# Up products of a two-layer trunk with the tokens stationary instead of the weights, and their turn by way of DRAM

## The chip, the core and the metric

The kernel runs on one core of a Trainium2 chip. The metric is the device time in microseconds from the start to the end of one execution. Every time here is of that kind, or of a stretch inside one profiled execution. TensorE multiplies: each matmul holds a 128 x 128 *stationary* tile and streams a *moving* tile of up to 512 columns past it, and the result lands in PSUM. VectorE and ScalarE work on SBUF and PSUM. SP issues the DMA transfers.

## The reference, cut to what matters

Two layers work on 256 tokens of width 2048. Layer 0 has forgetting attention, layer 1 dilated attention; each mixer and each MLP is preceded by an RMSNorm and adds into the residual stream. All data are float32.

```python
def sq_relu_mlp(h, w_up, w_down):
    a = jax.nn.relu(h @ w_up)          # (256, 2048) @ (2048, 8192)
    return (a * a) @ w_down            # (256, 8192) @ (8192, 2048)

for i in range(DEPTH):                 # DEPTH = 2
    h = rms_norm(x, mix_norm_g[i])
    x = x + mixer_i(h)                 # fox_attention, dilated_attention
    h = rms_norm(x, mlp_norm_g[i])
    x = x + sq_relu_mlp(h, mlp_w_up[i], mlp_w_down[i])
```

## The kernel before, in words

**Precision.** A float32 product is made of three products of rounded parts: every operand is split into a high part `hi` (a cast to the matmul's own 32-bit type `F32R`) and a rest `lo`, and hi·hi + hi·lo + lo·hi is summed in PSUM. Weights are split on the chip: `load` brings two row blocks of 128 x 512 (512 KB) into a `raw` tile; `split_part` casts them on ScalarE (L328, `wh`) and subtracts on VectorE (L329, `wl`). There are five `raw` tiles and five pairs of split tiles. A split is emitted when TensorE's program has used the oldest pair, and the next load when a `raw` tile has been split. The order of all weights is a list, `plan`, written to match the order of the products.

**Steps.** A *product* has 512 output columns and 16 steps, one for each 128 rows of the contraction. Each step ends in `jobs.tick()`. Everything that isn't a product's matmul (norms, the heads' softmax, what follows a product) is a generator; `yield 3` lets it go on three steps later, and `yield key` when another has set that key. `clear(n)` is n or n + 1, whichever makes the step odd. `need(key)` ticks on until the key is set. After each tick `pin` ties each engine's instructions to the order in which they were emitted, so this order is the program's order on every queue, SP's included. `in_group` runs some products in parts: with `PARTS` = (0, 12), (12, 16) and two products it does steps 0 to 11 of each, then 12 to 15 of each.

**Products with tokens stationary.** `product_steps` (L353) takes, per step and for each of two blocks of 128 tokens, three matmuls of 512 columns: token parts stationary, weight parts moving (L363 to L365). The result has tokens on the partitions, in two PSUM banks. All products but the MLP's up products are made so.

**The MLP.** `mlp` (L924) goes through four blocks of 2048 hidden columns: four up products, then four down products that contract these 2048 columns and add into `x` (`out_proj`, `add_chain`, L862). The down products want the hidden values with the hidden column on the partitions. Before, the up products deliver them so: `transposed_steps` (L417) holds 128 weight columns stationary and streams the tokens, per step four pairs of a matmul of 512 columns (weight `hi` against both token parts, L429) and one of 256 (weight `lo` against the tokens' `hi`, L433). The result lies in four banks, two of the pool `acc` and two of `sc` or `tp`. `up_chain` (L894) adds the halves of each bank (ScalarE copy L903, VectorE add L904), squares the positive part (L909) and splits it (L912, L913) into `aTh` and `aTl`, tiles of two chunks of 128 hidden columns. In the first block of each MLP the first two up products are a group, because the normalised tokens arrive piece by piece. The four down products follow one another undivided.

**Turning by way of DRAM.** Where tokens must be turned, `transposed_by_dma` (L455) and `qk_chain` (L538) turn 32 x 32 blocks on VectorE (`nc.vector.transpose`, L468, L563), write the 128 x 512 tile to DRAM in four transfers (`move`, L287) that put the blocks in their places, and read it back in one.

Of the kernel before, what the change touches and what calls it, by code (L numbers as in the profile page):

```python
# [17 lines left out]
P = 128  # L18
D = 2048
# [73 lines left out]
def trunk(ctx: ExitStack, tc, x, fox_w_in, fox_b_f, fox_q_gain, fox_k_gain, fox_w_out, dil_w_in,  # L93
# [296 lines left out]
    def last_product(keys, lhs, ready):  # L390
# [7 lines left out]
        for k, x in steps:  # L398
# [13 lines left out]
            if k < KC // 2 and x == len(parts) - 1:  # L412
                if k % W_SUB == W_SUB - 1:
                    split()
                jobs.tick()

    def transposed_steps(banks, keys, both, steps):  # L417


        for k in steps:  # L420
            jobs.need(keys(k))
            i = k % W_SUB
            hi, lo = splits[used[0]]
            tokens = both(k)
            for b in range(NC // P):
                col = slice(b * P, (b + 1) * P)

                def main(first, last):
                    nc.tensor.matmul(  # L429
                        banks[b], hi[:, i, col], in_turn(tokens.rearrange("p x s -> p (x s)"), P // 2), start=first, stop=last)  # L430

                def rest():
                    nc.tensor.matmul(banks[b][:, 0:S], lo[:, i, col], in_turn(tokens[:, 0, :], P // 2), start=False, stop=False)  # L433

                if k == 0:
                    main(True, False)
                    rest()
                else:
                    rest()
                    main(False, k == KC - 1)  # L440
            if i == W_SUB - 1:
                used[0] += 1
                split()
            jobs.tick()


    hT = {}
# [86 lines left out]
    def keys_h(tag):  # L534
        return lambda k: (tag, k // 2)
# [207 lines left out]
    def fox_head(j, hh, qT, kT, vt):  # L743
        h = 4 * j + hh
        at = ((2, 7, 12, 16) if j == 3 else (3, 8, 18, 22))[hh]
        yield ("fq", j)
        yield "gate"
        yield "mask"
        if hh:
            yield ("fk", j)  # L750
            yield at - 8

        bias = work.tile([P, 3 * P], F32, tag="bias", name=f"bias{h}", bufs=2)
        move(bias, negc[h:h + 1, :].to_broadcast([P, 3 * P]))
# [36 lines left out]


    def dil_head(q4, i, qTs, kTs, vt):
# [31 lines left out]
        yield ("dv", q4)  # L825
        pt_sb = yield from p_split(turned, f"d{h}")
        yield 2 if q4 == 3 else 4
        hi, lo = (act.tile([P, 2, S], F32R, tag=f"aT{x}", name=f"oTd{x}_{h}", bufs=KC // 2) for x in "hl")
        oT["d", h] = hi, lo
        yield from pv(pt_sb, vt, [i * S, i * S + P], [hi[:, 0, :], hi[:, 1, :]], [lo[:, 0, :], lo[:, 1, :]], f"d{h}", int(q4 < 3))  # L830
        jobs.done.add(("od", h))

# [44 lines left out]
            (nc.scalar if cols.start else nc.sync).dma_start(dst[:, :, cols.start // 2:cols.stop // 2], at)  # L877
        return ready

    def out_proj(keys, lhs, then=None, ready=None, scale=None, group=0):  # L880
        posts = [lambda acc, n=n: add_chain(acc, n, then, ready, scale) for n in range(NX)]
        if group:
            in_group(lambda n: sums(*(() if n < 2 else (ps_tp, "tp"))),
                     lambda acc, ks: product_steps(acc, keys, lhs, ks), posts[0:group], OUT_PARTS)
        for n in range(group, NX):
            if ready is not None and n == NX - 1:
                last_product(keys, lhs, final_add(n, scale))
            else:
                product(keys, lhs, posts[n])
# [1 line left out]
    def store(n, t):  # L891
        nc.sync.dma_start(out[0][t * P:(t + 1) * P, n * NC:(n + 1) * NC], xt[n][:, t, :])

    def up_chain(banks, key, n, aT):  # L894

        yield 0
        z = []
        for half in range(2):
            t = work.tile([P, 2, S], F32, tag="w", name=f"z_{key}_{n}_{half}", bufs=6)
            for i in range(2):  # L900
                bank = banks[half * 2 + i]
                at = halves(t[:, i, :], P // 2)
                nc.scalar.copy(at, by_column(bank[:, S:2 * S], P // 2))  # L903
                nc.vector.tensor_add(at, by_column(bank[:, 0:S], P // 2), at)  # L904
            z.append(t)
        for half in range(2):
            pr = n * 2 + half
            a = z[half]
            nc.vector.scalar_tensor_tensor(a, a, 0.0, a, ALU.max, ALU.mult)  # L909
            hi = act.tile([P, 2, S], F32R, tag="aTh", name=f"aTh_{key}_{pr}", bufs=KC // 2)  # L910
            lo = act.tile([P, 2, S], F32R, tag="aTl", name=f"aTl_{key}_{pr}", bufs=KC // 2)
            nc.scalar.copy(hi, a)  # L912
            nc.vector.tensor_sub(lo, a, hi.bitcast(F32))  # L913
            aT[pr] = (hi, lo)
            jobs.done.add((key, pr))
            yield 1

    def up_banks(key, n):

        other = (ps_sc, "sc") if n % 2 == 0 else (ps_tp, "tp")  # L920
        pools = (other, (ps_acc, "acc"))
        return [pool.tile([P, NC], F32, tag=tag, name=f"up_{key}_{n}_{tag}{i}") for pool, tag in pools for i in range(2)]

    def mlp(tag, **after):  # L924
        for b in range(4):
            key = f"{tag}a{b}"
            aT = {}
            posts = [lambda banks, n=n: up_chain(banks, key, n, aT) for n in range(4)]

            def steps(banks, ks):  # L930
                transposed_steps(banks, keys_h(tag), lambda k: hT[tag][k // 2][:, k % 2], ks)

            if b == 0:
                in_group(lambda n: up_banks(key, n), steps, posts[0:2])
            for n in range(0 if b else 2, 4):
                banks = up_banks(key, n)
                steps(banks, range(KC))
                jobs.spawn(posts[n](banks))
            out_proj(lambda k: (key, k // 2),
                     lambda k: (aT[k // 2][0][:, k % 2, :], aT[k // 2][1][:, k % 2, :]),  # L940
                     scale=tag, **(after if b == 3 else {}))

    def normed(tag, col, wait=lambda n: 2, later=lambda n: 2):
        ssp = norm_begin(tag)
# [62 lines left out]
    for j in range(4):  # L1007
# [11 lines left out]
        for hh in range(4):  # L1019
# [1 line left out]
        product(keys_h(tag), lhs_h(tag), lambda acc: v_chain(acc, tag, ("fv", j), vt))  # L1021

    out_proj(lambda k: ("of", k),
             lambda k: (oT["f", k // 2][0][:, k % 2, :], oT["f", k // 2][1][:, k % 2, :]),
             normed("n1", MLP_G), group=3)
    jobs.spawn(dilation_tables())
    mlp("n1", then=normed("n2", KC))
    dilated("n2")
    out_proj(lambda k: ("od", k // 2),
             lambda k: (oT["d", k // 2][0][:, k % 2, :], oT["d", k // 2][1][:, k % 2, :]),  # L1030
             normed("n3", MLP_G + KC), group=3)
    mlp("n3", ready=store)
    while jobs.live:
# [30 lines left out]
```

## Time and profile before

| | us |
|---|---|
| Median of three runs | 2143.05 (2142.60 to 2143.11) |
| Profiled execution | 2142.78 |
| Its span, first to last instruction | 2141.1 |
| One block's four up products (533.38 to 617.22) | 83.84 |
| One block's four down products (450.50 to 533.38) | 82.88 |
| TensorE busy | 2134.4 |
| VectorE busy | 1427.9 |
| ScalarE busy | 1094.9 |

The busy time of TensorE counts from a matmul's start to its modelled end, and these overlap; how fast it works is seen in the distances between starts. Idle time of VectorE, ScalarE or the DMA engines costs nothing by itself. A row of a group reads: line, engine, operation, result and operands, shape, count, then busy time, mean duration of one in ns, and the idle time before it with what ended that. A row of a wait reads: who, waited for whom, us in total, times, longest.

### The profile page before, as it was taken

The page shows a single profiled execution, that of the slowest core. Times are in us where ns is not written, and L with a number is a line of the kernel's source. Part 1 is how long each engine was busy: PE and PEld are TensorE (multiplying, and loading weights), DVE is VectorE, ACT ScalarE, POOL GpSimd, SP SyncE. Part 2 cuts the span into 40 slices and gives each one's busy share as a digit, 9 for nine tenths or more (in the row PEclk, how much of TensorE's full clock was granted, in tenths as well). Part 3 has the DMA queues.
Part 4 walks back from the last instruction along what each step waited for, and adds up shares of the span by engine and source line. Part 5 has one row for each costly group of instructions (what it writes and reads, how often), then busy time and mean ns, then how long its engine had stood idle before and what let it go on. Part 6 is the DMA issues. An engine that isn't in the chain of part 4 may idle for free.

```text
span 2141.1 us, 29878 instructions
## 1 busy us (share of the span) xinstructions
PE 2134.4 (100%) x11100; PEld 1900.5 (89%) x11100; DVE 1427.9 (67%) x1890; ACT 1094.9 (51%) x1523; POOL 49.8 (2%) x46
## 2 busy tenths in 40 slices
PE   9999999999999999999999999999999999999999
PEld 7888888988988998998888888888988988988988
DVE  6888876785665565566668787768655655665664
ACT  6565655644444453455555665646544543444442
POOL 2000000000000000000010010000000000000000
PEclk9999999999999999999999999999999999999999
DMA  7888877766666666657777776868666566666664
GB/s 253 258 260 271 251 243 243 235 212 202 191 211 204 197 206 205 201 188 255 244 238 231 245 242 216 260 202 277 203 204 201 190 214 205 197 206 202 201 212 143
DMA packets 315075, 471.97 MB, mean 220 GB/s; under 512 B 36440, under 2 KB 124848, under 8 KB 314928
## 3 DMA queue, kind: packets, MB, share of 16 engines
q1 hardware_dynamic: 314512, 469.66, 68.7%
q8 instruction: 87, 1.43, 0.3%
q14 instruction: 60, 0.49, 0.1%
q10 hardware_dynamic: 416, 0.39, 0.1%
HBM read 446.35 MB, written 23.62 MB: 219 GB/s over the span
## 4 chain that ended last, share of the span: by engine, by line
PE 99%; ACT 0%; DMA 0%; issue 0%; SPq 0%; DVE 0%; ACTq 0%
PE acc L364 21%; PE acc L363 21%; PE acc L365 21%; PE up_n3a_acc L429 5%; PE up_n1a_acc L429 5%; PE up_n3a_sc L429 3%; PE up_n3a_tp L429 3%; PE up_n1a_sc L429 3%; PE up_n1a_tp L429 3%; PE up_n1a_acc L433 3%; PE up_n3a_acc L433 3%; PE up_n1a_tp L433 1%; PE up_n1a_sc L433 1%; PE up_n3a_tp L433 1%; PE up_n3a_sc L433 1%; PE sc_d L672 0%
## 5 line engine op out<-in xcount | busy, mean ns | idle before, releaser
L329 DVE TENSOR_TENSOR wl<-raw,wh 128x1024 fp32r<-128x1024 f32 (+1 forms) x803 | 969.8, 1218 | 628.2 <-ACT wh L328 620.7
L328 ACT CAST wh<-raw 128x1024 fp32r<-128x1024 f32 (+1 forms) x803 | 830.5, 1044 | 863.5 <-PE acc L365 556.9
L363 PE MATMUL acc<-wh,hT_n 128*128 128x512 f32 x896 | 342.8, 383 | 0.4 <-ACT hT_n L506 0.3
L364 PE MATMUL acc<-wl,hT_n 128*128 128x512 f32 x896 | 339.8, 379 | 0.2 <-DVE wl L329 0.2
L365 PE MATMUL acc<-wh,hT_n 128*128 128x512 f32 x896 | 339.7, 379 | 0.0
L363 PE MATMUL acc<-wh,aTh_n1a 128*128 128x512 f32 x512 | 194.0, 379 | 0.0
L364 PE MATMUL acc<-wl,aTh_n1a 128*128 128x512 f32 x512 | 194.0, 379 | 0.0
L365 PE MATMUL acc<-wh,aTl_n1a 128*128 128x512 f32 x512 | 194.0, 379 | 0.0
L365 PEld LDWEIGHTS acc<-wh,hT_n 128*128 128x128 f32 x896 | 169.3, 189 | 24.2 <-DVE hT_n L507 0.2
L363 PEld LDWEIGHTS acc<-wh,hT_n 128*128 128x128 f32 x896 | 169.5, 189 | 23.4 <-ACT hT_n L506 0.6
L364 PEld LDWEIGHTS acc<-wl,hT_n 128*128 128x128 f32 x896 | 169.5, 189 | 23.1 <-DVE wl L329 0.8
L363 PE MATMUL acc<-wh,aTh_n3a 128*128 128x512 f32 x480 | 181.9, 379 | 0.0
L364 PE MATMUL acc<-wl,aTh_n3a 128*128 128x512 f32 x480 | 181.9, 379 | 0.0
L365 PE MATMUL acc<-wh,aTl_n3a 128*128 128x512 f32 x480 | 181.9, 379 | 0.0
L429 PE MATMUL up_n1a_acc<-hT_n,wh 128*128 128x512 f32 x512 | 181.6, 382 | 0.0
L429 PE MATMUL up_n3a_acc<-hT_n,wh 128*128 128x512 f32 x512 | 181.6, 382 | 0.0
L433 PE MATMUL up_n1a_acc<-hT_n,wl 128*128 128x256 f32 x512 | 139.6, 273 | 0.0
L433 PE MATMUL up_n3a_acc<-hT_n,wl 128*128 128x256 f32 x512 | 139.6, 273 | 0.0
L365 PEld LDWEIGHTS acc<-wh,aTl_n1a 128*128 128x128 f32 x512 | 96.8, 189 | 13.8
L364 PEld LDWEIGHTS acc<-wl,aTh_n1a 128*128 128x128 f32 x512 | 96.8, 189 | 13.7
L363 PEld LDWEIGHTS acc<-wh,aTh_n1a 128*128 128x128 f32 x512 | 96.8, 189 | 13.6
L429 PEld LDWEIGHTS up_n1a_acc<-hT_n,wh 128*128 128x128 f32 x512 | 96.8, 189 | 13.5
(681 smaller groups left out, 3159.9 us busy)
## 6 DMA issues: line engine op xcount, KB each, us to landing
raw<-in_mlp_w_up_dram SPq DMA_DIRECT2D x256, 512.0 KB, 4.3
raw<-in_mlp_w_down_dram SPq DMA_DIRECT2D x256, 512.0 KB, 4.2
raw<-in_dil_w_in_dram SPq DMA_DIRECT2D x192, 256.0 KB, 3.3
raw<-in_fox_w_in_dram SPq DMA_DIRECT2D x95, 512.0 KB, 5.0
raw<-in_fox_w_out_dram SPq DMA_DIRECT2D x32, 512.0 KB, 4.8
raw<-in_dil_w_in_dram SPq DMA_DIRECT2D x32, 512.0 KB, 4.4
raw<-in_dil_w_out_dram SPq DMA_DIRECT2D x32, 512.0 KB, 3.8
blocks_n<-turned_n SPq DMA_DIRECT2D x96, 64.0 KB, 2.4
```

What stands on the lines that cost most here:

```text
L328: nc.scalar.copy(hi[:, part, :], raw[:, part, :])
L329: nc.vector.tensor_sub(lo[:, part, :], raw[:, part, :], hi[:, part, :].bitcast(F32))
L363: nc.tensor.matmul(acc[t], ah[:, tok], hi, start=first, stop=False)
L364: nc.tensor.matmul(acc[t], ah[:, tok], lo, start=False, stop=False)
L365: nc.tensor.matmul(acc[t], al[:, tok], hi, start=False, stop=last)
L429: nc.tensor.matmul(banks[b], hi[:, i, col], in_turn(tokens.rearrange("p x s -> p (x s)"), P // 2), start=first, stop=last)
L433: nc.tensor.matmul(banks[b][:, 0:S], lo[:, i, col], in_turn(tokens[:, 0, :], P // 2), start=False, stop=False)
```

## The change

The up products are made by `product_steps`, as all others: tokens stationary, 512 columns of weights moving. Their result has tokens on the partitions, so `up_chain` now turns it. For each of the two token blocks it takes the positive part out of PSUM and squares it on ScalarE, turns 32 x 32 blocks on VectorE, writes to DRAM in four transfers and reads back in one, then splits it into tiles of four chunks (cast on ScalarE, subtraction on VectorE). The waits between these parts are counted in steps, some 19 from the product's end to the last subtraction. The heads' outputs `oT` share the tiles' tag, so they are kept by four chunks as well. In every block the first two of the four down products become a group in `PARTS`, and the list of weights follows. Only the `acc` pool's four banks serve the up products.

```diff
@@ add_mlp
-            for n in range(NX):
-                add(mlp_w_down[l], (b * D, (b + 1) * D), [(n * NC, NC)])
+            down = mlp_w_down[l][b * D:(b + 1) * D]
+            add_group(*((down, [(n * NC, NC)]) for n in range(2)))
+            for n in range(2, NX):
+                add(down, (0, D), [(n * NC, NC)])
@@
-    def transposed_steps(banks, keys, both, steps):
...
@@ fox_head (dil_head alike)
-        if ("f", h // 2) not in oT:
-            oT["f", h // 2] = tuple(
-                act.tile([P, 2, S], F32R, tag=f"aT{x}", name=f"oTf{x}_{h}", bufs=KC // 2) for x in "hl")
-        hi, lo = oT["f", h // 2]
-        yield from pv(pt_sb, vt, [hh * P], [hi[:, h % 2, :]], [lo[:, h % 2, :]], f"f{h}", int(j < 3))
+        if ("f", j) not in oT:
+            oT["f", j] = tuple(
+                act.tile([P, 4, S], F32R, tag=f"aT{x}", name=f"oTf{x}_{h}", bufs=KC // 4) for x in "hl")
+        hi, lo = oT["f", j]
+        yield from pv(pt_sb, vt, [hh * P], [hi[:, hh, :]], [lo[:, hh, :]], f"f{h}", int(j < 3))
@@ out_proj
-    def out_proj(keys, lhs, then=None, ready=None, scale=None, group=0):
+    def out_proj(keys, lhs, then=None, ready=None, scale=None, group=0, parts=OUT_PARTS):
...
-                     lambda acc, ks: product_steps(acc, keys, lhs, ks), posts[0:group], OUT_PARTS)
+                     lambda acc, ks: product_steps(acc, keys, lhs, ks), posts[0:group], parts)
@@
-    def up_chain(banks, key, n, aT):
...
+    def up_chain(acc, key, n, aT):
+
+        yield clear(0)
+        tiles = []
+        for t in range(NT):
+            a = work.tile([P, NC], F32, tag="w", name=f"a_{key}_{n}_{t}", bufs=6)
+            nc.scalar.activation(halves(a), by_column(acc[t]), AF.Relu)
+            nc.scalar.activation(a, a, AF.Square)
             yield 1
+            tile_ = work.tile([P, NC], F32, tag="w", name=f"turned_{key}_{n}_{t}", bufs=6)
+            blocks = dram.tile([4, 32, 4, P], F32, tag="blocks", name=f"blocks_{key}_{n}_{t}", bufs=4)
+            nc.vector.transpose(tile_.rearrange("p (j b r) -> p b j r", j=4, b=4),
+                                a.rearrange("p (b j c) -> p b j c", j=4, c=32))
+            for i in range(4):
+                move(blocks[:, :, i, :].rearrange("j c x -> c j x"),
+                     tile_[32 * i:32 * i + 32].rearrange("p (j x) -> p j x", j=4))
+            tiles.append((tile_, blocks))
+            yield 1
+        for tile_, blocks in tiles:
+            yield 2
+            move(tile_, blocks.rearrange("j c i x -> (j c) (i x)"))
+        yield clear(6)
+        hi, lo = (act.tile([P, 4, S], F32R, tag=f"aT{x}", name=f"aT{x}_{key}_{n}", bufs=KC // 4) for x in "hl")
+        for t in range(NT):
+            src = tiles[t][0].rearrange("p (i b r) -> p b i r", i=4, b=4)
+            ah, al = (x[:, :, t * P:(t + 1) * P].rearrange("p b (i r) -> p b i r", i=4) for x in (hi, lo))
+            nc.scalar.copy(ah, src)
+            yield 1
+            nc.vector.tensor_sub(al, src, ah.bitcast(F32))
+            yield 1
+        aT[n] = (hi, lo)
+        jobs.done.add((key, n))
@@ mlp
-            posts = [lambda banks, n=n: up_chain(banks, key, n, aT) for n in range(4)]
...
+            posts = [lambda acc, n=n: up_chain(acc, key, n, aT) for n in range(4)]
             if b == 0:
-                in_group(lambda n: up_banks(key, n), steps, posts[0:2])
+                in_group(lambda n: sums(), lambda acc, ks: product_steps(acc, keys_h(tag), lhs_h(tag), ks), posts[0:2])
             for n in range(0 if b else 2, 4):
-                banks = up_banks(key, n)
-                steps(banks, range(KC))
-                jobs.spawn(posts[n](banks))
-            out_proj(lambda k: (key, k // 2),
-                     lambda k: (aT[k // 2][0][:, k % 2, :], aT[k // 2][1][:, k % 2, :]),
-                     scale=tag, **(after if b == 3 else {}))
+                product(keys_h(tag), lhs_h(tag), posts[n])
+            out_proj(lambda k: (key, k // 4),
+                     lambda k: (aT[k // 4][0][:, k % 4, :], aT[k // 4][1][:, k % 4, :]),
+                     scale=tag, group=2, parts=PARTS, **(after if b == 3 else {}))
```

More of the change, by code (lines that the diff above doesn't have):

```diff
@@ L415, in last_product @@
                 jobs.tick()
-    def transposed_steps(banks, keys, both, steps):
[L420 to L444, printed above, removed]
     hT = {}
@@ L827, in dil_head @@
         yield 2 if q4 == 3 else 4
-        hi, lo = (act.tile([P, 2, S], F32R, tag=f"aT{x}", name=f"oTd{x}_{h}", bufs=KC // 2) for x in "hl")
-        oT["d", h] = hi, lo
+        if ("d", q4) not in oT:
+            oT["d", q4] = tuple(
+                act.tile([P, 4, S], F32R, tag=f"aT{x}", name=f"oTd{x}_{h}", bufs=KC // 4) for x in "hl")
+        hi, lo = (x[:, 2 * i:2 * i + 2] for x in oT["d", q4])
         yield from pv(pt_sb, vt, [i * S, i * S + P], [hi[:, 0, :], hi[:, 1, :]], [lo[:, 0, :], lo[:, 1, :]], f"d{h}", int(q4 < 3))
@@ L892, in store @@
         nc.sync.dma_start(out[0][t * P:(t + 1) * P, n * NC:(n + 1) * NC], xt[n][:, t, :])
-    def up_chain(banks, key, n, aT):
[L896 to L915, printed above, removed]
-            yield 1
@@ L918, in up_banks @@
[L918 to L922, printed above, removed]
+    def up_chain(acc, key, n, aT):
[5 more added lines that the diff above has]
+            nc.scalar.activation(a, a, AF.Square)
+            yield 1
+            tile_ = work.tile([P, NC], F32, tag="w", name=f"turned_{key}_{n}_{t}", bufs=6)
[21 more added lines that the diff above has]
+        jobs.done.add((key, n))
@@ L1023, in trunk @@
     out_proj(lambda k: ("of", k),
-             lambda k: (oT["f", k // 2][0][:, k % 2, :], oT["f", k // 2][1][:, k % 2, :]),
+             lambda k: (oT["f", k // 4][0][:, k % 4, :], oT["f", k // 4][1][:, k % 4, :]),
              normed("n1", MLP_G), group=3)
@@ L1029, in trunk @@
     out_proj(lambda k: ("od", k // 2),
-             lambda k: (oT["d", k // 2][0][:, k % 2, :], oT["d", k // 2][1][:, k % 2, :]),
+             lambda k: (oT["d", k // 4][0][:, k % 4, :], oT["d", k // 4][1][:, k % 4, :]),
              normed("n3", MLP_G + KC), group=3)
```

2 lines of the change are left out of this document (removed).

## The prediction

> **What bounds the kernel now.** I read the page's busy table and its slices first, to see whether any stretch has an engine other than TensorE near its limit.
>
> ```profile
> span 2141.1 us, 29878 instructions
> ...
> PE 2134.4 (100%) x11100; PEld 1900.5 (89%) x11100; DVE 1427.9 (67%) x1890; ACT 1094.9 (51%) x1523; POOL 49.8 (2%) x46
> ...
> PE   9999999999999999999999999999999999999999
> ...
> PEclk9999999999999999999999999999999999999999
> DMA  7888877766666666657777776868666566666664
> ...
> PE 99%; ACT 0%; DMA 0%; issue 0%; SPq 0%; DVE 0%; ACTq 0%
> ```
>
> TensorE is at nine tenths or more in all 40 slices, at full clock, and it is 99% of the chain that ended last. VectorE, ScalarE and the DMA engines have room on average. A busy share could still hide short gaps, so the waits of TensorE came next, for the whole run:
>
> ```profile
> PE spare L146 <- DVE zeros L142: 1.5, 1, 1.5
> PE ps_g_mix L165 <- DMA g_mix<-in_mix_norm_g_dram: 0.8, 1, 0.8
> PE acc L363 <- ACT hT_n L506: 0.3, 1, 0.3
> PE sc_f L672 <- DVE fkT_0l L592: 0.3, 1, 0.3
> PE acc L364 <- DVE wl L329: 0.2, 1, 0.2
> ```
>
> That is all of it: 3.1 us, none of it in an MLP. So TensorE is never late for data there; only fewer or cheaper matmuls can save time, and every new wait on it would be paid in full. What a matmul costs is its distance from start to start, not its recorded duration (durations overlap). So I asked for windows from the first matmul of a stage to the first of the next. The columns are: stretch, its length, then busy time and instruction count of TensorE, its weight loads, VectorE, ScalarE, GpSimd, then the granted clock, the DMA share and GB/s.
>
> ```profile
> 1033.54:1147.50 113.96, 113.96 (x529) 99.79 (x528) 78.29 (x108) 67.98 (x99) 8.21 (x5) 1.00 0.78 244
> 100.00:240.00 140.00, 140.00 (x689) 123.73 (x688) 114.18 (x196) 85.55 (x145) 8.19 (x5) 1.00 0.85 257
> 450.50:533.38 82.88, 82.88 (x385) 72.58 (x384) 51.49 (x57) 35.49 (x38) 0.00 (x0) 1.00 0.64 209
> 533.38:617.22 83.84, 83.84 (x513) 77.06 (x512) 51.74 (x58) 39.62 (x50) 0.00 (x0) 1.00 0.65 202
> ```
>
> Row three is one block's four down products: 64 steps, 384 matmuls of 512 columns (the count includes the next stage's first), 82.88/384 = 215.8 ns each, 1.295 us a step. Row four is one block's four up products: also 64 steps, but 512 matmuls, 256 of 512 columns and 256 of 256, 83.84/256 = 327.5 ns a pair, 1.310 us a step. Row one is the opening of the dilated mixer: 528 matmuls of `product_steps` with the normalised tokens `hT` stationary and the weights streamed, exactly the form that the up products will have. 113.96/528 = 215.8 ns again, although that stretch carries the turn-by-DRAM traffic of `qk_chain`.
>
> **The change part by part.** *Up products on TensorE.* Each of 512 steps (2 layers x 4 blocks x 4 products x 16) loses 4 pairs and gains 6 matmuls: 4 x 327.5 = 1310.0 ns against 6 x 215.8 = 1295.0 ns. A block goes from 83.84 to 82.88 us, and there are 8: 8 x 0.96 = **7.7 us off the path**. The multiply work (columns streamed) is equal, 3072 a step in both; only the small excess of the pairs goes. That excess sits in these starts:
>
> ```profile
> 533.38 0.38 PE L429 MATMUL up_n1a_sc<-hT_n,wh 128*128 128x512 f32 x1
> 533.60 0.27 PE L433 MATMUL up_n1a_sc<-hT_n,wl 128*128 128x256 f32 x1
> 533.71 0.38 PE L429 MATMUL up_n1a_sc<-hT_n,wh 128*128 128x512 f32 x1
> ```
>
> 0.22 and 0.11 us; a pair of 327.5 ns is 3.8 ns more than one and a half of 215.8 (323.7). The Trainium skill ("TensorE: Matmul & The Clock Gate", Back-to-back issue gap) gives a warm matmul N/2.4 + 2.5 ns. By that rule a pair would be 325.0 ns and the save 4 x 325.0 - 6 x 215.8 = 5.2 ns a step, 2.7 us in all; the trace agrees on 215.8 and has 2.5 ns more on the pair, so the rows decide.
>
> *The up product's tail, off the path.* Removed and added per up product, from one block's groups and the nearest rows:
>
> ```profile
> L904 DVE TENSOR_TENSOR z_n1a<-up_n1a_acc,z_n1a 128x256 f32<-128x256 f32 x6 | 2.2, 416 | 0.0
> L909 DVE SCALAR_TENSOR_TENSOR z_n1a<-z_n1a 128x512 f32<-128x512 f32 x6 | 4.1, 684 | 0.0
> L913 DVE TENSOR_TENSOR aTl_n1a<-z_n1a,aTh_n1a 128x512 fp32r<-128x512 f32 x6 | 4.2, 692 | 4.1 <-ACT aTh_n1a L912 4.1
> L903 ACT COPY z_n1a<-up_n1a_acc 128x256 f32<-128x256 f32 x6 | 2.0, 392 | 0.0
> L912 ACT CAST aTh_n1a<-z_n1a 128x512 fp32r<-128x512 f32 x6 | 3.7, 618 | 10.5 <-DVE z_n1a L909 10.5
> L468 DVE STREAM_TRANSPOSE turned_n<-x x24: 667/690/714, 347.0 to 1481.8; 128x512 f32<-128x512 f32 x24
> L544 ACT ACTIVATE sq_('fk', 1)_0_1387<-acc,rstd_n x1: 681/681/681, 124.3 to 124.3; 128x512 f32<-128x512 f32 x1
> L592 DVE TENSOR_TENSOR dkT_2l<-dkT_2w,dkT_2h x4: 500/502/504, 1143.0 to 1387.7; 128x256 fp32r<-128x256 f32 x4
> L328 ACT CAST wh<-raw 128x1024 fp32r<-128x1024 f32 x32 | 32.9, 1046 | 33.7 <-PE up_n1a_acc L429 29.7 <-ACT wh L328 2.4 <-PE acc L365 1.5
> L329 DVE TENSOR_TENSOR wl<-raw,wh 128x1024 fp32r<-128x1024 f32 x33 | 39.9, 1224 | 29.3 <-ACT wh L328 29.2
> ```
>
> VectorE loses 4 x 0.416 + 2 x 0.684 = 3.0 us and gains 2 x 0.690 = 1.4 us of transposes. Its two subtractions now read in pieces of 32: between 0.69 (L913) and 2 x 0.50 (L592, half the size) each; I take 0.9. ScalarE loses 4 x 0.39 = 1.6 and gains two Relu out of PSUM and two squares at 0.62 to 0.68, 2.6 us. Its two casts in pieces lie between 0.62 and 1.05, and I take 0.8. With the eight weight splits (1.05 and 1.22 us) ScalarE is then at about 12.6 and VectorE at about 13 of a product's 20.7 us. Cost on the path: nothing. The cover is the five split weight tiles ahead: ScalarE's idle time before a cast is put down to TensorE (29.7 of 33.7 us in L328's row), which means the split waits for a tile to come free, ten steps (13 us) before use. Relu has no row here; from both sides it is 0.39 (L903, half size) to 0.68 + 1.28 us (a table load, last fence), and even the upper end stays on an engine that is 51% busy.
>
> *The DMA queue.* Each up product adds 8 writes of 64 KB and 2 reads of 256 KB, 320 issues in all, to SP's queue, which also issues the weights.
>
> ```profile
> blocks_n<-turned_n SPq DMA_DIRECT2D x96, 64.0 KB, 2.4
> turned_n<-blocks_n SPq DMA_DIRECT2D x24, 256.0 KB, 5.7
> qn_('fq', 0)_1_641<-blocks_('fq', 0)_1_644 SPq DMA_DIRECT2D x1, 256.0 KB, 7.1
> raw<-in_mlp_w_up_dram SPq DMA_DIRECT2D x256, 512.0 KB, 4.3
> DMA to landing us min/median/max: 2.5/4.3/8.9
> L287 SPq DMA_DIRECT2D blocks_n<-turned_n x96: 302/432/1530, 347.7 to 1485.2; - x96
> SPq L308 <- DVE wl L329: 1151.9, 564, 7.8
> ```
>
> Ten issues at 0.43 us are 4.3 us of 20.7. Behind a write that waits for its transpose, or a read that waits for its writes, stand weight loads; who waits for those is the cast five raw tiles (13 us) later, and behind it TensorE another 13 us later. SP itself now mostly waits for tiles to come free (1151.9 us), so it has room. Bytes: a block adds 4 x 2 x 512 KB = 4.2 MB to 16.8 MB, and 21.0 MB in 82.88 us are 253 GB/s. The window 100 to 240 ran 257 GB/s at a DMA share of 0.85, with per three products two `qk_chain` turns, four heads' turns and bias rows, and TensorE lost nothing to it. Cost: nothing.
>
> *The chain's length against the down products in parts.* Counted in steps of 1.295 us from the end of a block's last up product: Relu and square at 1 and 3, transposes and writes at 2 and 4, reads at 7 and 9, casts at 15 and 17, subtractions at 16 and 18. ScalarE and VectorE run up to 1.05 + 1.22 us behind the step (the split comes first), so the tile is whole at about 18 x 1.295 + 2.3 + 0.9 = 26.5 us. Down product 0 takes parts 0..11, then product 1 its 0..11; the last up product's tile is first read at step 24, 31.1 us. Margin 4.6 us. The product before it ends 16 steps earlier and is read at step 8: 4.5 us. The second read starts about 12.7 + 0.4 us (behind the load of step 8) and lands 5.7 to 7.1 us later, by 20.2; its cast can't come before step 17's place, 23 us. So from its issue at 13.1 a read has 9.9 us before it delays the cast and, with the margin of 4.6, 14.5 before TensorE waits; the slowest weight load took 8.9. Cost: nothing.
>
> *PSUM banks.* Up now uses the four `acc` banks alone. Tightest: after the first block's group, the third up product needs product 0's second bank at 4 steps plus 3 matmuls, 5.8 us; its Relu at step 3 ends about 2.6 + 1.05 + 0.7 = 4.4. Down product 2 needs down 0's banks 5.2 us after that ends: split (1.05 + 1.22) and two adds make 3.8 us by the rows below. Each holds by over a microsecond; missed by one, they would cost 2 and 8 us.
>
> ```profile
> L862 DVE SCALAR_TENSOR_TENSOR x<-acc,rstd_n,x x62: 741/744/747, 473.6 to 2119.5; 128x512 f32<-128x512 f32 x62
> L954 ACT ACT_TABLE_LOAD  x1: 1283/1283/1283, 1.3 to 1.3; - x1
> ```
>
> *The rest.* Four heads' outputs in one tile instead of two changes no matmul; if reads waited for the whole tile it could cost 0 to 2 us at the two output projections (a cast and a subtraction late); I take 0. The parts move the adds of down products 0 and 1 to steps 28 and 32 from 16 and 32; the mixer that follows starts on the last add, which stays.
>
> Sum, against the profiled execution: 2142.78 us (span 2141.1) - 7.7 = 2135.1. The median of the runs is 0.27 us above that execution, so the forecast is **2135.4 us**.
>
> **The rivals.** *Slower: the turn through DRAM is late.* Place: down product 0 or 1 at step 12, in 8 blocks. TensorE waits there if a read takes over 14.5 us. It decides from (7.7 + 4.3)/8 = 1.5 us a block, a landing of 16 us. At 17 us it costs 2.5 x 8 = 20 us and the time is 2155. For it: the DMA share climbs from 0.65 towards 0.85. Against it: the rows at 0.85 have landings of 5 to 7 us.
>
> *No gain: the excess belongs to the up stage, not to the pairs.* Then the 384 matmuls take 83.84/384 = 218.3 ns and the time stays at 2143. For it: pairs are seen in that stage alone. Against it: row one of the windows, with the same `hT` tiles, at 215.8. The skill's gap rule named above would land near it too, at 2140.4.
>
> *Part of the gain lost to banks or tiles:* one missed margin of 1 us at the adds costs 8, at the two groups 2; together with the 2 us of the projections the time lies between 2137 and 2143.
>
> **How the numbers follow.** What a measurement of this kernel can tell from no change is about 0.2%, 4.3 us. The forecast has 0.77: 2134 to 2137 (noise of the median, the tile's bound). Part lost 0.09, over half of it still beyond 4.3 us; no gain 0.04; late turn 0.10. Faster 0.82, same 0.08, slower 0.10. The range runs from 2134 to 2140, which leaves out the late turn, the case without gain and the upper part of the lost gain.
>
> **What would show it.** Right: a block's up stage of 82.9 us with 384 matmuls; no new row among TensorE's waits; VectorE's share in an up window lower, ScalarE's higher, DMA near 250 GB/s; one table load. Wrong: a wait of `acc` for `aTh`, `aTl` or a cast at L363 to L365 in the first down product; a weight split waiting for a DMA; or a matmul distance in the up stage over 216 ns.

## The result, and the profile after

The changed kernel takes 2136.8 us (median of 7 runs, 2135.53 to 2137.05); the kernel before took 2143.11 us in 7 runs (2142.60 to 2144.78). The ratio is 0.9968, 95% interval 0.9956 to 0.9979: faster by 0.3%, clear of no change. In the later sets, beside the experiments, the kernel before had medians of 2144.1 to 2144.6 us (15, 9 and 13 runs) and a second set of the changed kernel 2136.7 us (5 runs), ratio 0.9964 (0.9952 to 0.9977).

The page of the changed kernel's profiled execution (2137.05 us), the lines that answer to those of before:

```profile
span 2135.3 us, 28026 instructions
...
PE 2129.3 (100%) x10076; PEld 1866.8 (87%) x10076; DVE 1386.4 (65%) x1762; ACT 1132.7 (53%) x1523; POOL 49.8 (2%) x46
...
DMA  7889877886786786787777776868876876776874
...
PE 99%; ACT 0%; DMA 0%; issue 0%; DVE 0%; SPq 0%; ACTq 0%
```

1024 matmuls fewer, the same full TensorE, VectorE a little less busy, ScalarE a little more, the DMA engines fuller where the MLPs are. All the waits of TensorE, and then the windows of the first two blocks' up and down stages (columns as in the prediction):

```profile
PE spare L146 <- DVE zeros L142: 1.5, 1, 1.5
PE ps_g_mix L165 <- DMA g_mix<-in_mix_norm_g_dram: 0.8, 1, 0.8
PE sc_f L645 <- DVE fkT_0l L565: 0.3, 1, 0.3
```

```profile
368.64:451.52 82.88, 82.88 (x385) 72.58 (x384) 61.59 (x92) 55.07 (x90) 1.19 (x3) 1.00 0.89 287
451.52:534.40 82.88, 82.88 (x385) 72.58 (x384) 50.43 (x54) 37.23 (x39) 0.00 (x0) 1.00 0.71 217
534.40:617.28 82.88, 82.88 (x385) 72.58 (x384) 46.66 (x44) 42.65 (x49) 0.00 (x0) 1.00 0.79 241
617.28:700.16 82.88, 82.88 (x385) 72.58 (x384) 46.83 (x44) 37.22 (x39) 0.00 (x0) 1.00 0.71 216
```

No wait of TensorE was added anywhere. An up stage now takes as long as a down stage, 82.88 us against 83.84, in every one of the eight blocks: 8 x 0.96 = 7.7 us. The two profiled executions differ by 5.7 us only (2142.78 and 2137.05): 2.0 us were lost again before the first MLP, which starts at 368.64 us here and started at 366.66 us before, though nothing ahead of it computes differently. The starts of the first products show where:

```profile
7.03 0.38 PE L364 MATMUL acc<-wl,hT_n 128*128 128x512 f32 x1
7.25 0.47 PE L365 MATMUL acc<-wh,hT_n 128*128 128x512 f32 x1
7.55 0.38 PE L363 MATMUL acc<-wh,hT_n 128*128 128x512 f32 x1
7.77 0.38 PE L364 MATMUL acc<-wl,hT_n 128*128 128x512 f32 x1
```

```profile
7.80 0.63 PE L366 MATMUL acc<-wl,hT_n 128*128 128x512 f32 x1
8.23 0.63 PE L367 MATMUL acc<-wh,hT_n 128*128 128x512 f32 x1
8.66 0.63 PE L365 MATMUL acc<-wh,hT_n 128*128 128x512 f32 x1
9.08 0.63 PE L366 MATMUL acc<-wl,hT_n 128*128 128x512 f32 x1
```

The first four rows are the kernel before, at 0.22 us from start to start (once 0.30); the second four are the changed kernel at the same place, at 0.43, half the rate. That ends at about 12 us.

### The profile page after: what moved, and what is told of

It reads as the page before. It is cut to its first block, busy times and chain, and to the rows that moved or that the text cites. A ratio compares the mean times of both kernels' runs of the same rounds, so it can differ in the third digit from the quotient of the medians.

```text
span 2135.3 us, 28026 instructions
## 1 busy us (share of the span) xinstructions
PE 2129.3 (100%) x10076; PEld 1866.8 (87%) x10076; DVE 1386.4 (65%) x1762; ACT 1132.7 (53%) x1523; POOL 49.8 (2%) x46
## 4 chain that ended last, share of the span: by engine, by line
PE 99%; ACT 0%; DMA 0%; issue 0%; DVE 0%; SPq 0%; ACTq 0%
PE acc L365 32%; PE acc L366 32%; PE acc L367 32%; PE sc_d L645 0%; PE sc_f L645 0%; PE po_f L594 0%; PE po_d L594 0%; PE sc_d L642 0%; PE acc L409 0%; PE acc L410 0%; PE acc L411 0%; PE ptx_n L477 0%; PE pf L656 0%; DMA g_mix<-in_mix_norm_g_dram 0%; PE po_d L595 0%; PE po_f L595 0%
## 5 line engine op out<-in xcount | busy, mean ns | idle before, releaser
L365 PE MATMUL acc<-wh,hT_n 128*128 128x512 f32 x1920 | 731.7, 381 | 0.1
L366 PE MATMUL acc<-wl,hT_n 128*128 128x512 f32 x1920 | 728.5, 379 | 0.0
L367 PE MATMUL acc<-wh,hT_n 128*128 128x512 f32 x1920 | 728.4, 379 | 0.0
L367 PEld LDWEIGHTS acc<-wh,hT_n 128*128 128x128 f32 x1920 | 363.3, 189 | 51.6
L365 PEld LDWEIGHTS acc<-wh,hT_n 128*128 128x128 f32 x1920 | 363.6, 189 | 50.6 <-ACT hT_n L479 0.5
L366 PEld LDWEIGHTS acc<-wl,hT_n 128*128 128x128 f32 x1920 | 363.5, 189 | 50.2 <-DVE wl L331 0.3
L367 PEld LDWEIGHTS acc<-wh,aTl_n3a 128*128 128x128 f32 x480 | 90.7, 189 | 12.9
L366 PEld LDWEIGHTS acc<-wl,aTh_n3a 128*128 128x128 f32 x480 | 90.7, 189 | 12.9
L365 PEld LDWEIGHTS acc<-wh,aTh_n3a 128*128 128x128 f32 x480 | 90.7, 189 | 12.8
L365 PE MATMUL acc<-wh,oTdh 128*128 128x512 f32 x128 | 48.9, 382 | 0.0
L365 PE MATMUL acc<-wh,oTfh 128*128 128x512 f32 x128 | 48.9, 382 | 0.0
```

The lines of the kernel that those rows point to most:

```text
L365: nc.tensor.matmul(acc[t], ah[:, tok], hi, start=first, stop=False)
L366: nc.tensor.matmul(acc[t], ah[:, tok], lo, start=False, stop=False)
L367: nc.tensor.matmul(acc[t], al[:, tok], hi, start=False, stop=last)
```

## The experiments

**Only the parts of the down products.** The kernel before with this edit:

```diff
-            for n in range(NX):
-                add(mlp_w_down[l], (b * D, (b + 1) * D), [(n * NC, NC)])
+            down = mlp_w_down[l][b * D:(b + 1) * D]
+            add_group(*((down, [(n * NC, NC)]) for n in range(2)))
+            for n in range(2, NX):
+                add(down, (0, D), [(n * NC, NC)])
...
-                     scale=tag, **(after if b == 3 else {}))
+                     scale=tag, group=2, parts=PARTS, **(after if b == 3 else {}))
```

> The kernel before, with only the first two down products of each block in parts; up products, their tail and all else as before. My theory (the whole gain is the matmuls of the up stage, and the parts are only cover): no change, 2143 us within 1 us, an up window of 83.84 us and no new wait of TensorE. Rival (the parts themselves are worth part of the gain, or cost some through the PSUM banks of down product 2): 2137 to 2140 us, or 2151 us with waits of 1 us in 8 places.

Measured: 2144.09 us (10 runs) against 2144.11 (15 runs), ratio 1.0001 (0.9992 to 1.0011); an up window of 83.84 us, a down window of 82.88, no new wait. The parts give nothing and cost nothing by themselves; the banks of down product 2 are free in time. My theory holds.

**Without the parts.** The changed kernel with the opposite edit (down products in one piece each).

> The changed kernel with the down products undivided again. The last up product's tile is then read at step 12, 15.5 us after that product's end, instead of at step 24. By my count of the chain it is whole at 26.5 us if its later pieces keep their places, so TensorE would wait 11 us in each of 8 blocks: 2137 + 88 = 2225 us. The pieces are emitted without matmuls between them once the program waits for them, so the reads' landing (by 18.8 to 20.2 us, then a cast and a subtraction, 1.7 us) may set it instead: 5 to 6.5 us a block, 2177 to 2189 us. Rival (the chain is much shorter than I count): under 2145 us.

Measured: 2179.05 us (one run), 42 us over the changed kernel, 3 to 7 us a block. Two rows of its waits of TensorE (two more, for `aTl`, have 2.6 and 1.9 us), and the place in the third block's first down product at step 12:

```profile
PE acc L364 <- ACT aTh_n1a L894: 8.9, 7, 3.0
PE acc L364 <- ACT aTh_n3a L894: 7.4, 7, 1.7
```

```profile
807.92 0.38 PE L366 MATMUL acc<-wh,aTl_n1a 128*128 128x512 f32 x1
809.96 0.48 PE L364 MATMUL acc<-wh,aTh_n1a 128*128 128x512 f32 x1 [1.65 <-ACT aTh_n1a L894]
...
811.30 0.75 PE L366 MATMUL acc<-wh,aTl_n1a 128*128 128x512 f32 x1 [0.64 <-DVE aTl_n1a L896]
812.30 0.79 PE L364 MATMUL acc<-wh,aTh_n1a 128*128 128x512 f32 x1 [0.25 <-ACT aTh_n1a L894]
812.89 0.63 PE L365 MATMUL acc<-wl,aTh_n1a 128*128 128x512 f32 x1
813.31 0.63 PE L366 MATMUL acc<-wh,aTl_n1a 128*128 128x512 f32 x1
```

The time is that of the second expected case (2177 to 2189 us), but not for its reason alone. Once the program waits, the later pieces do follow one another, and the cast of the tile's second half waits 1.72 us for the landing of its read (at 811.63 us). But the waits are 2.5 us in this block, not 5 to 6.5, and 20.8 us in all. Most of the other half of the 42 us is that matmuls start 0.43 us apart after the waits, as in the opening. The column of the granted clock shows it, 0.50 for 3.4 us in this block, and 1.00 around the same place of the second block:

```profile
811.38:814.79 3.41, 3.16 (x7) 2.15 (x8) 0.69 (x1) 0.62 (x1) 0.00 (x0) 0.50 0.53 178
636.00:646.00 10.00, 7.70 (x34) 5.86 (x33) 4.38 (x5) 4.06 (x5) 0.00 (x0) 1.00 0.79 260
```

That the total fell into the expected range is therefore partly luck. The parts are the cover that the turn needs, worth 42 us.

**Without the turn.** The changed kernel, the transposes and all DMA of the up products taken out:

```diff
-            tile_ = work.tile([P, NC], F32, tag="w", name=f"turned_{key}_{n}_{t}", bufs=6)
-            blocks = dram.tile([4, 32, 4, P], F32, tag="blocks", name=f"blocks_{key}_{n}_{t}", bufs=4)
-            nc.vector.transpose(...)
-            for i in range(4):
-                move(blocks[:, :, i, :]...)
-            tiles.append((tile_, blocks))
+            tiles.append((a, None))
...
-            move(tile_, blocks.rearrange("j c i x -> (j c) (i x)"))
```

> The changed kernel without the turn: the transposes on VectorE and all DMA of the up products left out, the squared values split straight from where ScalarE left them (so the hidden values are not turned, which is left out of the computation); the steps are kept. My theory (the turn is hidden whole): 2136.8 us within 1 us, the same as the changed kernel, with a DMA share of about 0.65 in an up window. Rival (the turn takes part of the gain back): below 2136 us by what it takes.

Measured: 2136.68 us (6 runs), ratio to before 0.9967 (0.9955 to 0.9978), with an up window of 82.88 us at a DMA share of 0.65 and 203 GB/s. The turn's 320 transfers and 64 transposes cost nothing on the path.

**The casts four and eight steps later.** The changed kernel with `yield clear(10)` and with `yield clear(14)` in place of `yield clear(6)` in `up_chain`.

> The changed kernel with the casts and subtractions of every up product four steps (5.2 us) later. By my count the tile is whole 4.6 us before it is read, so this oversteps the margin by 0.6 us: 0 to 1 us of wait in each of 8 blocks, 2137 to 2145 us. If the margin is larger than counted: 2136.8 us and no wait. If it is much smaller: 1.3 us a block for each step that it is short, 2150 us and more.

> The changed kernel with the casts and subtractions of every up product eight steps (10.4 us) later. With four steps only the first block of the first MLP waited, 1 us, so the other seven blocks have more than 5.2 us to spare. If they have the 4.6 us that I counted plus what the emission gives back once the program waits, TensorE waits 4 to 6 us a block: 2137 + 32 to 48 us = 2169 to 2185 us. Rival (the spare time is over 10 us everywhere but in the first block): under 2150 us.

Measured: 2136.53 us with four steps and 2163.97 with eight (one run each). With four, one block of the eight lost 1.0 us, the first of the first MLP, and in it TensorE waited for the tile of up product 2 at step 8 of the first down product, not for the last one at step 24:

```profile
PE acc L367 <- DVE aTl_n1a L897: 0.7, 1, 0.7
```

```profile
449.92:533.81 83.89, 83.15 (x385) 72.50 (x384) 50.64 (x54) 37.74 (x40) 0.00 (x0) 1.00 0.72 220
616.69:699.57 82.88, 82.88 (x385) 72.58 (x384) 46.81 (x44) 37.74 (x40) 0.00 (x0) 1.00 0.70 217
```

Four steps are 5.2 us, so the other seven blocks have more than that to spare. How much is seen in the changed kernel itself, in the last subtractions into the tiles of up products 2 and 3 of its second block, whose up stage ended at 617.28 us, and in the first of the two with the delay of four steps, whose up stage ended at 616.69:

```profile
622.31 0.69 DVE L897 TENSOR_TENSOR aTl_n1a<-turned_n1a,aTh_n1a 128x512 fp32r<-128x512 f32 x1
643.01 0.68 DVE L897 TENSOR_TENSOR aTl_n1a<-turned_n1a,aTh_n1a 128x512 fp32r<-128x512 f32 x1
626.89 0.68 DVE L897 TENSOR_TENSOR aTl_n1a<-turned_n1a,aTh_n1a 128x512 fp32r<-128x512 f32 x1
```

The tiles are whole 5.7 and 26.4 us after the up stage's end, and read by the last matmul of steps 8 and 24, at 11.4 and 32.2: 5.7 us to spare for each. With four steps more the first is whole at 10.9, still in time. In the first block of the first MLP it was whole at 6.0 in the changed kernel, 5.5 us ahead, but at 12.3 with the delay: there four steps had become 6.3 us. The prediction counted 4.5 us.

Eight steps are 10.4 us and cost 27 us in all: 2.2 us in four of the eight blocks and 3.9 to 6.0 in the others. Every block waits at step 8. In seven the waits are the same, 0.8 and 0.6 us; in three of these, and in the first, the granted clock then falls to 0.50 for 3.4 us. The rows of the second and the fourth block (0.72 over the 6 us of the window):

```profile
634.00:640.00 6.00, 4.60 (x19) 3.50 (x20) 2.40 (x3) 2.18 (x3) 0.00 (x0) 1.00 0.79 273
971.00:977.00 6.00, 5.28 (x15) 4.04 (x16) 1.56 (x3) 1.07 (x2) 0.00 (x0) 0.72 0.72 256
```

The total lies between the two expected cases. It does not measure the spare time: in the second block the earlier tile was whole at 13.5 us, not at 5.7 + 10.4 = 16.1, because the program, once it waits, emits the pieces without matmuls between them.

**The writes to DRAM doubled.** The changed kernel with a second copy of each turned tile, written behind the first:

```diff
+            again = dram.tile([4, 32, 4, P], F32, tag="again", name=f"again_{key}_{n}_{t}", bufs=4)
+            for i in range(4):
+                move(again[:, :, i, :].rearrange("j c x -> c j x"),
+                     tile_[32 * i:32 * i + 32].rearrange("p (j x) -> p j x", j=4))
```

> The changed kernel with every turned tile written to DRAM a second time (8 more transfers of 64 KB for each up product, 16.8 MB in all); the second copy is never read. My theory (landings have 7 us to spare): 2136.8 us within 1 us, DMA share in an up window up by about 0.1, no wait of TensorE. Rival (DMA queue or bandwidth near its limit): a wait of TensorE for a weight split or for aTh in the down products, 8 blocks x 1 us and more, 2145 us and up.

Measured: 2141.33 us (one run). This expectation missed: two blocks waited, the first of each MLP, and the other six did not.

```profile
450.36:534.91 84.55, 83.43 (x386) 72.34 (x385) 53.15 (x59) 38.43 (x41) 0.00 (x0) 1.00 0.79 252
1551.80:1638.46 86.66, 83.68 (x385) 72.41 (x384) 47.26 (x45) 38.52 (x41) 0.00 (x0) 1.00 0.79 251
534.91:617.79 82.88, 82.88 (x386) 72.58 (x385) 46.55 (x44) 42.58 (x48) 0.00 (x0) 1.00 0.79 237
```

The down stages of those two (first two rows) took 84.55 and 86.66 us instead of 82.88. The DMA share of an up window did not rise (third row, 0.79 as before the edit); that of the second block's down window did, from 0.71 to 0.77. The transfers did not land later (128 first writes of the first MLP at a median of 3.0 us, reads at 5.2, against 3.5 and 5.3 in the changed kernel), so bandwidth is not what ran out. What was added is SP's time, 8 more issues of 0.44 us a product, ahead of the reads; the first block is the one where two up products end four steps apart and both turn at once. SP's rows for up product 2 of that block, its first writes and its first read, with the second copy and without:

```profile
442.11 2.71 SPq L289 DMA_DIRECT2D blocks_n1a<-turned_n1a  x4
451.88 0.48 SPq L289 DMA_DIRECT2D turned_n1a<-blocks_n1a  x1
```

```profile
437.75 1.78 SPq L289 DMA_DIRECT2D blocks_n1a<-turned_n1a  x4
443.03 0.41 SPq L289 DMA_DIRECT2D turned_n1a<-blocks_n1a  x1
```

The first MLP began at 367.48 us in the one and at 368.64 in the other, so the writes were issued 5.5 us later and the read 10.0 us later, and the tile was whole 6.9 us later, past its 5.5 us to spare. In the second block it was 2.6 us late, and the spare time covered that. So the lateness is in SP's issuing, not in the transfers. No run adds issues without bytes, so the two are told apart by these rows alone.

**Where the excess of the old form sits: streaming patterns.** Three runs ask whether the 3.8 ns that a pair had over one and a half wide matmuls come from the interleaved order in which the tokens were streamed. First the kernel before with the tokens in plain order:

```diff
-                        banks[b], hi[:, i, col], in_turn(tokens.rearrange("p x s -> p (x s)"), P // 2), start=first, stop=last)
+                        banks[b], hi[:, i, col], tokens.rearrange("p x s -> p (x s)"), start=first, stop=last)
...
-                    nc.tensor.matmul(banks[b][:, 0:S], lo[:, i, col], in_turn(tokens[:, 0, :], P // 2), start=False, stop=False)
+                    nc.tensor.matmul(banks[b][:, 0:S], lo[:, i, col], tokens[:, 0, :], start=False, stop=False)
```

> The kernel before, with the tokens of transposed_steps streamed in their plain order instead of the interleaved one, and the banks taken out in plain order. If the 3.8 ns that a pair has over one and a half matmuls of 215.8 ns come from the interleaved pattern of the 512-column matmul, a pair falls from 327.5 to 325.0 ns or less: 2048 pairs x 2.5 ns = 5.1 us, so 2138 us. If they come from there being two matmuls for one and a half (a fixed cost for each), the time stays at 2143 us. If plain order streams slower, the time goes up, and the interleaving is worth what it goes up by.

Measured: 2190.06 us, ratio 1.0217 (1.0201 to 1.0232). An up window takes 89.61 us, a pair 350 ns. Plain order is dearer by 22.5 ns a pair; the interleaving earns 46 us in this kernel. It is not the source of the excess, at least not by being there at all. Then the number of pieces, in the changed kernel (with `apart` = P // 2 for the up products alone) and in the one before:

```diff
-            hi, lo = (in_turn(w[:, i, :]) for w in splits[used[0]])
+            hi, lo = (in_turn(w[:, i, :], apart) for w in splits[used[0]])
```

```diff
-                        banks[b], hi[:, i, col], in_turn(tokens.rearrange("p x s -> p (x s)"), P // 2), start=first, stop=last)
+                        banks[b], hi[:, i, col], in_turn(tokens.rearrange("p x s -> p (x s)"), P), start=first, stop=last)
```

> The changed kernel with the weights of the up products streamed in the pattern that the tokens had before: four pieces of 64 pairs, [2,64,4], instead of one of 256 pairs, [2,256,1]; the Relu reads the banks accordingly. Theory P (the excess belongs to the streaming pattern): each of the 3072 matmuls takes 218.3 ns instead of 215.8, an up window takes 83.8 us again and the whole gain is gone, 2144 us. Theory F (the excess is a fixed cost of there being eight matmuls a step instead of six, as my sum has it): 82.9 us a window and 2136.7 us.

> The kernel before with the tokens streamed in half as many pieces: two of 128 pairs for the 512-column matmul and one of 128 pairs for the 256-column one, the banks taken out accordingly. Theory P: the 512-column matmul falls from 218.3 to between 215.8 and 217 ns and the pair to 324 to 326 ns, 2048 x 1.5 to 3.5 ns = 3 to 7 us off, 2137 to 2141 us. Theory F: 2144 us, no change.

Measured: 2136.64 us (ratio 0.9963, 0.9948 to 0.9977) and 2144.05 us (ratio 0.9999, 0.9989 to 1.0008). The up windows are 82.89 us in the first and 83.84 in the second, as without the edits. Theory P falls: neither more pieces on the new form nor fewer on the old change anything.

**Where the excess sits: the widths.** The kernel before, with the matmuls of `transposed_steps` in another form in each block (the comments are added here):

```diff
+            for bs in ([range(4)] if form == 1 else [[b] for b in range(4)]):
...
+                    for b in bs:
+                        rest(b)        # form 0: 512 columns instead of 256
+                    for b in bs:
+                        main(b, False, k == KC - 1)        # form 2: two of 256 columns (not at the first and last step)
```

> The kernel before, with the up matmuls of each block in another form, the same in both MLPs: block 0 makes both of a pair 512 columns wide (the rest against both token parts, one product more); block 1 makes the four 256-column matmuls of a step together and then the four 512-column ones; block 2 makes three of 256 columns for each pair; block 3 as before. Theory A (each 512-column matmul with weights stationary and tokens moving takes 218.3 ns, whatever stands beside it): up windows of 512 x 218.3 = 111.8 us in block 0, 83.84 in block 1. Theory B (2.5 ns over the columns for each matmul, and 2.5 more for a 512-column one only beside a 256-column one): 110.5 us in block 0, about 83.4 in block 1. Block 2: 12 x 109.2 ns a step, 83.9 us, if a matmul of 256 columns keeps its 109.2 ns when all are so short; more, if the loading of the stationary tile bounds it. Whole time 2197 to 2200 us.

Measured: 2200.85 us (one run). The up windows of blocks 0 to 3 of the first MLP, and part of a step of block 1 (rows merged two by two; starts in the first column):

```profile
368.06:478.56 110.50, 110.50 (x513) 96.80 (x512) 67.79 (x105) 53.00 (x91) 1.19 (x3) 1.00 0.58 189
561.44:645.28 83.84, 83.84 (x513) 76.99 (x512) 51.74 (x58) 39.57 (x50) 0.00 (x0) 1.00 0.64 201
728.16:813.68 85.52, 85.52 (x737) 84.67 (x736) 51.74 (x58) 39.60 (x50) 0.00 (x0) 1.00 0.63 198
896.56:980.40 83.84, 83.84 (x513) 77.11 (x512) 51.73 (x58) 39.63 (x50) 0.00 (x0) 1.00 0.62 200
```

```profile
562.31 0.39 PE L440 MATMUL up_n1a_sc<-hT_n,wl 128*128 128x256 f32 x2
562.53 0.39 PE L440 MATMUL up_n1a_acc<-hT_n,wl 128*128 128x256 f32 x2
```

Block 0: 110.50/512 = 215.8 ns for every matmul, with weights stationary and tokens moving, so theory A falls. Block 1: 83.84 us still, though only two places in a step have unlike neighbours, so theory B falls in its second half. What is left, and fits all four: a matmul of 256 columns takes (83.84 us - 256 x 215.8 ns)/256 = 111.7 ns, summed over a stage, wherever it stands, and one of 512 takes 215.8. The 256-column ones alone are 0.22 us a pair in the last fence, 111 ns each. Block 2, with 56 steps of twelve and eight of the old form: 56 x 12 x 111.7 ns + 8 x 1310 ns = 85.5 us, as measured. The expected 83.9 us held only if a short matmul kept 109.2 ns; that block 2 took 1.6 us more, twice, is why the whole came out above the 2197 to 2200 us expected. Two of 256 columns cost 223.4 ns against 215.8 for one of 512. Why the short one takes 111.7 ns is not shown: every matmul here has its own weight load, and these were busy for 84.67 of 85.52 us in block 2 (99%) and 96.80 of 110.50 in block 0 (88%), so the load may set the pace where all matmuls are short.

**The opening.** The changed kernel with `wake(8)` instead of `wake(6)`, and beside it the changed kernel once more.

> The changed kernel with eight matmuls on zeros ahead of the first product instead of six. The profiled run of the changed kernel made its first matmuls at 427 ns from start to start until 12 us, that of the kernel before at 216 ns from 7 us on, and its runs lie in two groups, 2135.5 to 2135.7 and 2136.5 to 2137.1 us. If the gap of TensorE at 4 to 5 us is what lets the slow start last longer, filling it brings all runs to the lower group: 2135.6 us in the median. If not, the two groups stay, with the median at 2136.8 us.

> The changed kernel itself once more, beside e7 on the same chip: 2136.8 us in the median, two groups of runs; its profile shows in which group the profiled run falls, by the distance of the matmuls between 7 and 12 us.

Measured: 2136.11 us (2135.58 to 2137.10) and 2136.70 us (2135.97 to 2137.14), five runs each. The ranges overlap, so the edit is not shown to help, and the two groups of runs did not come back as such. In the profile of the second the first matmuls started 0.43 us apart until 11 us; in that of the first they started 0.22 us apart from 7 us on, and then TensorE waited for weights instead:

```profile
10.97 0.48 PE L365 MATMUL acc<-wh,hT_n 128*128 128x512 f32 x1 [0.83 <-ACT wh L330]
```

The first MLP began at 367.71 us with it and at 368.54 without.

## Why the prediction was right, point by point

- **Up products on TensorE, 7.7 us.** Right to the last digit: 83.84 to 82.88 us in all eight blocks.
- **The sum.** The forecast was 2135.4 us and the median is 2136.8. The MLPs gave what was forecast. What the sum lacked is the opening, which the prediction took for fixed: in the profiled execution 2142.78 - 7.7 + 2.0 = 2137.1, and 2137.05 was measured. That the median's 1.4 us have the same source is inferred. The first MLP began between 366.5 and 368.6 us in the profiled executions, at 366.47 and 368.22 in two with the old up products (parts alone, plain order), and at 367.04 and 368.64 in two with the new (casts four steps later, the changed kernel). The execution on which the sum was made (366.66) lay at the early end. This scatter of 2 us is wider than the 1.5 us that the forecast allowed on either side, so that the median still fell inside 2134 to 2137 is partly luck. In the set of the second measurement the medians differ by 7.9 us (2144.55 and 2136.70).
- **Where the excess sits.** The prediction read it as "the small excess of the pairs" and left it there. By the run with the widths, the excess is that of the short matmul: 111.7 ns, 3.8 more than half of a wide one (107.9). The starts in a pair (218 and 109 ns) showed part of the short one's price at its neighbour. The Trainium skill's rule for a single warm matmul (TensorE: Matmul & The Clock Gate, Back-to-back issue gap, N/2.4 + 2.5 ns) agrees with 215.8; an estimate by it for 256 columns is 109.2 ns, against 111.7 measured with a stationary tile for each.
- **The tail off the path.** Right: leaving the turn out changes nothing. The sizes were near: VectorE 46.66/4 = 11.7 us a product (13 forecast), ScalarE 42.65/4 = 10.7 (12.6). The groups of the second block's up window in the changed kernel show why:

```profile
L897 DVE TENSOR_TENSOR aTl_n1a<-turned_n1a,aTh_n1a 128x512 fp32r<-128x512 f32 x4 | 2.7, 685 | 0.0
...
L875 ACT ACTIVATE a_n1a<-acc 128x512 f32<-128x512 f32 x6 | 3.5, 592 | 0.0
L895 ACT CAST aTh_n1a<-turned_n1a 128x512 fp32r<-128x512 f32 x5 | 3.1, 614 | 0.0
```

  The pieces of 32 cost nothing extra (685 and 614 ns, as for whole rows), and Relu takes 592 ns with no second table load.
- **The DMA queue.** Right that it is hidden; 241 GB/s at 0.79 in the up window, part of the last product's share falling into the down window (216). The first block has 287 GB/s at 0.89, more than the 253 forecast; it had 241 at 0.71 before, where the second block had 202, so the prediction took the traffic of a lighter block. Landings:

```profile
blocks_n1a<-turned_n1a SPq DMA_DIRECT2D x128, 64.0 KB, 3.5
turned_n1a<-blocks_n1a SPq DMA_DIRECT2D x32, 256.0 KB, 5.3
```

- **The chain's length.** The prediction counted the last tile whole at 26.5 us; it was, at 26.4. The margin counted was 4.5 us for the tile before the last and 4.6 for the last; both have 5.7 in the second block, because the late half of a tile is read 1.1 us into its step. In the first block of the first MLP the earlier tile has 5.5. The prediction looked for the danger of a late turn at the last tile's step 12; with the chain delayed, it was the tile before, read at step 8, that TensorE waited for.
- **PSUM banks and parts.** Right: no wait, and the parts alone cost nothing.
- **The rivals.** The late turn did not come. Its price was sized too low: "every new wait on it would be paid in full" leaves out the clock, and without the parts 20.8 us of waits came with a loss of 42. With the writes doubled it was SP's issuing that made the reads late, not the landing that this rival named. The case without gain rested on an excess that belongs to the stage; the up window of 82.88 us, block 0 of the forms and the four pieces show that it doesn't.

## What to carry to other kernels

Where TensorE is full, compare the forms of a product by the distance between starts over a whole stage, and prefer matmuls of the full 512 columns: half as many columns took more than half the time here, 111.7 ns against 215.8. A turn by way of DRAM that takes some 20 steps is free as long as the order of the products leaves that many steps before its result is read; count that margin for every tile that is read early, check it against the trace, and delay the chain by a little more than it. Keep the turn from TensorE's path also because waits of 1.4 to 2.5 us were followed, in some blocks, by matmuls at half rate, and the loss was then 1.5 to 3 times the wait that the rows list.

## What the runs showed of the hardware that had not been expected

- The order in which the moving operand is read matters: tokens in plain order cost 350 ns a pair against 327.5 for the same tokens in pairs from two places. With pairs, the number of pieces (1, 2 or 4) made no difference.
- A matmul of 256 columns with its own stationary tile takes 111.7 ns, and 215.8 for 512, summed over a stage, whatever its neighbours are.
- Short waits cost more than their length. Without the parts, after TensorE had waited 2 to 2.5 us within some 4 us, the granted clock was 0.50 for 3.4 us and matmuls started 0.43 us apart in one block (at 812 us), and not in another (at 642 us). With the casts eight steps later the same waits of 0.8 and 0.6 us were followed by a granted clock of 0.50 for 3.4 us in three blocks and not in four.
- The same half rate holds at the start of an execution, until before 7 us in one profile and 12 us in another. The column of the granted clock shows 1.00 there because the trace has no clock record before 5.16 us in the first and 12.12 us in the second; in the opening it is the distance of the starts that tells it.
